# The seven forms of a swiglu's input at seven different rests of 512 bytes

## The chip, the cores and the metric

The kernel runs on one core of a Trainium2 chip. The metric is the device time of one execution in microseconds, the median over runs. A profile of one execution shows, for each engine, when every instruction ran. The engines are TensorE (PE for matmuls, PEld for the loads of their weights), VectorE (DVE), ScalarE (ACT), GpSimd (POOL) and SyncE (SP, which here only issues DMAs).

## The reference

A small streaming trunk: 256 tokens of width 2048, two layers, everything float32. Layer 0 mixes the tokens by gated linear attention, layer 1 by a sparse attention over a latent; after each mixer comes a swiglu. The change concerns the swiglus alone.

```python
def swiglu(h, w1, w3, w2):
    return (jax.nn.silu(h @ w1) * (h @ w3)) @ w2

def reference(x, ...):
    for i in range(DEPTH):              # DEPTH = 2
        h = rmsnorm(x, norm_mix[i])
        y = gla_mixer(h, ...) if i % 2 == 0 else dsa_mixer(h, ...)
        x = x + y
        x = x + swiglu(rmsnorm(x, norm_ffn[i]), ffn_w1[i], ffn_w3[i], ffn_w2[i])
    return rmsnorm(x, norm_final)
```

The matrices w1 and w3 are 2048 x 5632, w2 is 5632 x 2048.

## The kernel before

**Precision.** Each float32 product is made of three matmuls in the type float32r. A tile is split into a high part (a cast) and a low part (the rest), and the product is hi x wh + hi x wl + lo x wh. In every matmul the activations are the stationary operand, 128 x 128, and the weights the moving one, 128 x 512. So each group of three matmuls loads weights (in TensorE's sense) three times, from hi, hi and lo, and streams wh, wl and wh.

**Weights.** A block of 512 x 512 weights comes by a DMA of 1 MB into a buffer (raw, or one of v0, v1, v2, g3), ScalarE casts it to wh (line 137 in the feed-forward layers) and VectorE subtracts to get wl (line 138). There are three buffers each of wh and wl.

**Blocks of a swiglu.** The 5632 columns of w1 and w3 are 11 blocks of 512. Seven of them are made by a scheme of seven products (`pair`): h is cut into four parts by tokens and by width, and combinations of these parts, the *forms*, are multiplied with combinations of the weights. The forms are A11, F7, F5, A12, F6, F3 and N22. Each has a high and a low tile of 128 x 8 x 128 elements, 4096 bytes in each partition, made once per layer by `NormF.split` and kept for the layer. In `product` one pair of w blocks is multiplied with one form by 24 matmuls (line 397). The other four blocks use A11, F7, A12 and N22 only: one at the start (`plain`, line 468), three in pieces between the products (`plain_steps`, line 498). The second matrix w2 follows in pieces in between (`pieces`, lines 554 to 556). Their stationary tiles are g0 to g2.

**Where tiles stand.** A tile pool lays its tiles one behind another in the order in which their tags first appear. A pool named fz0 or fz1, opened for each swiglu, holds v0, the forms, the scratch tiles s1, y and w of the sums, v1 and v2. Every one of its tiles is a multiple of 2048 bytes in a partition, and the pool starts at byte 140800, which is 275 x 512. So in the kernel before all of them start at a multiple of 512 bytes: their *rest* of 512 is 0. The same holds for raw, wh, wl, g0 to g3 and for hh and hl, the high and low tiles of the mixers' inputs (lines 205 to 207). Tiles with other rests are found in the attention layer: its latent cth, ctl and its keys kih, kil at rest 192, its queries qh, ql at rest 320. With cth or ctl as stationary operand, the latent values (pv, lines 1027 to 1029, 512 columns) read whv and wlv, which lie in the buffers of wh and wl; the scores (psi, lines 920 to 922, and psl, lines 1046 to 1048, 256 columns) read qh and ql against kih, kil, cth and ctl.

**Order.** The order on each engine is that in which the code issues; what is put aside (transposes, scores and the like) is drawn into the stream of matmuls by `tick`.

Of the kernel before, what the change touches and what calls it, by code (L numbers as in the profile page):

```python
# [12 lines left out]
F32 = mybir.dt.float32  # L13
# [6 lines left out]
P = 128  # L20
# [35 lines left out]
def trunk(  # L56
# [219 lines left out]
    class NormF(Norm):  # L276
# [9 lines left out]
        def split(self, name, c, src, neg=False):  # L286
            if name not in self.forms:
                self.forms[name] = [self.pool.tile([P, 8, P], F32R, tag=f"{q}{name}", bufs=1, name=f"{q}{name}")
                                    for q in ("fh", "fl")]
            hi, lo = (z[:, 4 * c:4 * c + 4, :] for z in self.forms[name])  # L290
            if neg:
                nc.scalar.mul(hi, src, -1.0)
                nc.vector.scalar_tensor_tensor(lo, src, -1.0, hi.bitcast(F32), op0=ALU.mult, op1=ALU.subtract)
            else:
                nc.scalar.copy(hi, src)
                nc.vector.tensor_sub(lo, src, hi.bitcast(F32))
# [878 lines left out]
```

## Time and profile before

| | us |
|---|---|
| median of 2 runs | 2232.94 |
| lowest, highest | 2232.69, 2233.19 |
| profiled execution, from its first to its last instruction (span) | 2232.1 |
| layer 0, mixer and its output (0 to 395) | 395 |
| layer 0, swiglu (395 to 1080) | 685 |
| layer 1, mixer and its output (1080 to 1565) | 485 |
| layer 1, swiglu (1565 to 2160) | 595 |
| last block of w2 and the final norm | 72 |

The bounds of the stages are those of the first and last instructions of their lines, rounded. Of the profiled execution the profile gives the span alone; no time of its own stands beside it. [...] In rows of groups, the number behind x is the count, then come the busy time in us, the mean duration in ns and the idle time before.

### The profile page before, as it was taken

How to read it: one execution, taken by the hardware profiler on the slowest of the kernel's cores; microseconds unless marked ns; L12 is line 12 of the kernel's file. 1: busy time of each engine (PE TensorE's matmuls, PEld its weight loads, DVE VectorE, ACT ScalarE, POOL GpSimd, SP SyncE). 2: the span in 40 equal slices, each digit the busy share in tenths (PEclk: the TensorE clock that was granted, in tenths of full speed). 3: DMA queues.
4: the chain of work that ended last, by engine and by line, in shares of the span. 5: the costliest groups of instructions: out<-in, count | busy, mean ns of one | idle time of the engine just before them, and what ended most of it. 6: DMA issues, size and time to landing. Idle time of an engine off the chain costs nothing.

```text
span 2232.1 us, 25168 instructions
## 1 busy us (share of the span) xinstructions
PE 2217.3 (99%) x10247; PEld 1837.9 (82%) x10247; DVE 1577.6 (71%) x1282; ACT 1172.2 (53%) x1046; POOL 100.1 (4%) x147
## 2 busy tenths in 40 slices
PE   9999999999999999999999999999999999999998
PEld 8888888888888888888888888888888888888887
DVE  6546546778878878876555755556887887887874
ACT  5545445555555555555444444446555555555553
POOL 0000000000000000000100000000000000000000
PEclk9999999999999999999999999999999999999999
DMA  8555475597897898795554554467679779779763
GB/s 292 172 170 181 132 232 177 202 272 244 253 265 242 251 269 244 241 245 192 179 182 144 180 173 159 163 200 244 205 217 293 244 225 305 229 225 305 232 202 110
DMA packets 250547, 484.96 MB, mean 217 GB/s; under 512 B 8072, under 2 KB 20704, under 8 KB 250304
## 3 DMA queue, kind: packets, MB, share of 16 engines
q1 hardware_dynamic: 219856, 423.33, 55.1%
q0 software_dynamic: 29568, 58.72, 15.2%
q8 instruction: 80, 1.31, 0.2%
q10 hardware_dynamic: 1008, 1.31, 0.2%
q14 instruction: 35, 0.29, 0.0%
HBM read 481.20 MB, written 2.12 MB: 217 GB/s over the span
## 4 chain that ended last, share of the span: by engine, by line
PE 94%; DVE 2%; issue 1%; ACT 1%; DMA 1%; POOL 0%; POOLq 0%; ACTq 0%; DVEq 0%
PE acc L397 23%; PE acc L205 12%; PE acc L207 12%; PE acc L206 12%; PE half L498 11%; PE down L555 5%; PE down L556 5%; PE down L554 5%; PE acc L468 3%; PE tr L219 1%; DVE wl L138 1%; DMA g<-in_ffn_w 1%; PE trq L906 0%; PE po L765 0%; PE tr L253 0%
## 5 line engine op out<-in xcount | busy, mean ns | idle before, releaser
L196 DVE TENSOR_TENSOR wl<-raw,wh 128x2048 fp32r<-128x2048 f32 (+3 forms) x161 | 349.8, 2175 | 306.6 <-ACT wh L195 306.5
L137 ACT CAST wh<-raw 128x2048 fp32r<-128x2048 f32 x187 | 358.0, 1915 | 371.2 <-PE down L556 134.9
L138 DVE TENSOR_TENSOR wl<-raw,wh 128x2048 fp32r<-128x2048 f32 x187 | 427.1, 2289 | 160.2 <-ACT wh L137 159.9
L195 ACT CAST wh<-raw 128x2048 fp32r<-128x2048 f32 (+3 forms) x161 | 292.0, 1816 | 267.0 <-PE acc L207 211.1
L205 PE MATMUL acc<-wh,hh 128*128 128x512 f32 (+3 forms) x832 | 325.5, 391 | 0.0
L207 PE MATMUL acc<-wh,hl 128*128 128x512 f32 (+3 forms) x832 | 317.4, 381 | 0.0
L206 PE MATMUL acc<-wl,hh 128*128 128x512 f32 (+3 forms) x832 | 316.3, 380 | 0.6 <-DVE wl L196 0.6
L138 DVE TENSOR_TENSOR wl<-v,wh 128x2048 fp32r<-128x2048 f32 x102 | 232.8, 2288 | 34.2 <-ACT wh L137 34.1
L137 ACT CAST wh<-v 128x2048 fp32r<-128x2048 f32 x102 | 195.4, 1916 | 94.8 <-PE acc L397 54.9
L554 PE MATMUL down<-wh,g 128*128 128x512 f32 x512 | 200.0, 391 | 0.0
L556 PE MATMUL down<-wh,g 128*128 128x512 f32 x512 | 199.4, 389 | 0.0
L555 PE MATMUL down<-wl,g 128*128 128x512 f32 x512 | 199.3, 389 | 0.0
L206 PEld LDWEIGHTS acc<-wl,hh 128*128 128x128 f32 x832 | 156.7, 188 | 29.6 <-issue 1.7
L207 PEld LDWEIGHTS acc<-wh,hl 128*128 128x128 f32 x832 | 156.3, 188 | 29.5
L205 PEld LDWEIGHTS acc<-wh,hh 128*128 128x128 f32 x832 | 156.5, 188 | 28.4 <-issue 1.9
L397 PE MATMUL acc<-wh,fhF 128*128 128x512 f32 x448 | 175.1, 391 | 0.0
L397 PE MATMUL acc<-wh,flF 128*128 128x512 f32 x448 | 174.8, 390 | 0.0
L397 PE MATMUL acc<-wl,fhF 128*128 128x512 f32 x448 | 174.7, 390 | 0.0
L205 PE MATMUL acc<-wh,g 128*128 128x512 f32 x424 | 167.4, 395 | 0.0
L206 PE MATMUL acc<-wl,g 128*128 128x512 f32 x424 | 165.6, 391 | 0.0
L207 PE MATMUL acc<-wh,g 128*128 128x512 f32 x424 | 165.5, 390 | 0.0
L555 PEld LDWEIGHTS down<-wl,g 128*128 128x128 f32 x512 | 96.1, 188 | 20.1 <-DVE wl L138 0.4
(311 smaller groups left out, 3602.3 us busy)
## 6 DMA issues: line engine op xcount, KB each, us to landing
raw<-in_ffn_w SPq DMA_DIRECT2D x208, 1024.0 KB, 6.3
raw<-in_dsa_w_in SPq DMA_DIRECT2D x48, 1024.0 KB, 4.9
v<-in_ffn_w SPq DMA_DIRECT2D x42, 1024.0 KB, 8.3
raw<-in_gla_w_in SPq DMA_DIRECT2D x40, 1024.0 KB, 5.0
v<-in_ffn_w POOLq DMA_DIRECT2D x40, 1024.0 KB, 8.9
raw<-in_gla_w_out SPq DMA_DIRECT2D x16, 1024.0 KB, 5.0
g<-in_ffn_w POOLq DMA_DIRECT2D x16, 1024.0 KB, 12.5
raw<-in_dsa_w_out SPq DMA_DIRECT2D x16, 1024.0 KB, 4.9
```

The costliest lines, as they stand in the source:

```text
L137: nc.scalar.copy(wh, raw)
L138: nc.vector.tensor_sub(wl, raw, wh.bitcast(F32))
L195: a = nc.scalar.copy(wh[:, sl, :n], raw[:, sl, :n])
L196: v = nc.vector.tensor_sub(wl[:, sl, :n], raw[:, sl, :n], wh[:, sl, :n].bitcast(F32))
L205: nc.tensor.matmul(acc[t][:, :n], hi[:, k, ts_], wh[:, k, :n], start=start, stop=False)
L206: nc.tensor.matmul(acc[t][:, :n], hi[:, k, ts_], wl[:, k, :n], start=False, stop=False)
L207: nc.tensor.matmul(acc[t][:, :n], lo[:, k, ts_], wh[:, k, :n], start=False, stop=last)
L397: nc.tensor.matmul(acc, l_[:, k, :], r_[:, j, :], start=start and k == i == 0, stop=stop and k == 7 and i == 2, skip_group_check=not start)
L498: nc.tensor.matmul(acc[bank], l_[:, k, :], r_[:, j, :], start=start and k == i == 0, stop=stop and k == 7 and i == 2, skip_group_check=not ...
L554: nc.tensor.matmul(acc[t], hi[:, k, ts_], wh[:, k, :], start=start, stop=False)
L555: nc.tensor.matmul(acc[t], hi[:, k, ts_], wl[:, k, :], start=False, stop=False)
L556: nc.tensor.matmul(acc[t], lo[:, k, ts_], wh[:, k, :], start=False, stop=last)
```

## The change

When a form is first made, a tile of 16 float32 (64 bytes in a partition) that nothing uses is allocated behind its high and low tile, except behind the last form.

```diff
@@ class NormF, split(self, name, c, src, neg=False)
             if name not in self.forms:
                 self.forms[name] = [self.pool.tile([P, 8, P], F32R, tag=f"{q}{name}", bufs=1, name=f"{q}{name}")
                                     for q in ("fh", "fl")]
+                if len(self.forms) < 7:
+                    self.pool.tile([P, 16], F32, tag=f"rest{name}", bufs=1, name="rest")
             hi, lo = (z[:, 4 * c:4 * c + 4, :] for z in self.forms[name])
```

The instructions, their order on each engine and their waits are the same as before. What differs is where tiles start, in bytes of a partition (rest of 512 in brackets):

| tile | before | after |
|---|---|---|
| v0 | 140800 (0) | 140800 (0) |
| A11 high, low | 148992, 153088 (0) | the same (0) |
| s1 | 157184 (0) | 157248 (64) |
| F7 | 159232, 163328 (0) | 159296, 163392 (64) |
| v1 | 167424 (0) | 167552 (128) |
| y | 175616 (0) | 175744 (128) |
| F5 | 177664, 181760 (0) | 177792, 181888 (128) |
| w | 185856 (0) | 186048 (192) |
| A12 | 187904, 192000 (0) | 188096, 192192 (192) |
| F6 | 196096, 200192 (0) | 196352, 200448 (256) |
| F3 | 204288, 208384 (0) | 204608, 208704 (320) |
| N22 | 212480, 216576 (0) | 212864, 216960 (384) |
| v2 | 220672 (0) | 221056 (384) |
| wh, wl, raw, g0 to g3 | rest 0 | the same |

## The prediction

> **What bounds the kernel now.** I read the page first, then the busy time by stage, then the matmul rows of the feed-forward blocks, and last the chain of waits and the rows of single matmuls, since the change can only act through the cost of one instruction.
>
> ```profile
> span 2232.1 us, 25168 instructions
> PE 2217.3 (99%) x10247; PEld 1837.9 (82%) x10247; DVE 1577.6 (71%) x1282; ACT 1172.2 (53%) x1046; POOL 100.1 (4%) x147
> PEclk9999999999999999999999999999999999999999
> PE 94%; DVE 2%; issue 1%; ACT 1%; DMA 1%; POOL 0%; POOLq 0%; ACTq 0%; DVEq 0%
> ```
>
> TensorE is busy all the time, at the full granted clock, and the chain that ended last is TensorE for 94%. The two windows in which the feed-forward layers run:
>
> ```profile
> core 0: us, PE busy (x) PEld busy (x) DVE busy (x) ACT busy (x) POOL busy (x), PEclk, DMA share, GB/s
> 395.00:1080.00 685.00, 684.91 (x3076) 566.02 (x3075) 544.47 (x354) 378.77 (x268) 37.92 (x33) 1.00 0.81 241
> 1565.00:2160.00 595.00, 594.28 (x2659) 491.33 (x2658) 491.77 (x306) 330.69 (x210) 36.35 (x28) 1.00 0.83 246
> ```
>
> In 685 us TensorE has 0.1 us without a matmul in flight; VectorE is at 79%, ScalarE at 55%, the DMA engines at 81%. So a nanosecond on each matmul there is a nanosecond on the end, until VectorE or the DMAs are what is waited for, and those have about a fifth left.
>
> What one matmul costs shows in the chain, where a run of equal pieces is merged:
>
> ```profile
> 439.45 5.44 PE acc L397 x24
> 511.20 10.88 PE half L498 x48
> ```
>
> 10.88 us / 48 = 226.7 ns from one matmul to the next. A row's duration is longer because neighbours overlap; in an undisturbed run it is 389 ns, so a duration is about 162 ns over the spacing, and differences of durations are differences of spacing.
>
> **The change part by part.** It adds seven pads to the pool and no instruction: every engine has the same rows in the same order with the same waits, and no tile changes its size. Only the start addresses move. A11 stays at rest 0 of 512 bytes; F7 goes to 64, F5 to 128, A12 to 192, F6 to 256, F3 to 320, N22 to 384 (high and low half alike). With them move the scratch tiles s1, y and w and the weight buffers v1 (rest 128) and v2 (384). The moving operands of all these matmuls, wh and wl, stay at rest 0.
>
> How many matmuls read a moved form. The first three rows are those of line 397 (count, then shortest, median and longest duration in ns, first and last start), the others groups by shape (count, then busy us and mean ns). The views drop the digits: fhF is F7, F5, F6 and F3, fhA is A11 and A12, fhN is N22.
>
> ```profile
> L397 PE MATMUL acc<-wh,fhF x448: 387/389/481, 451.2 to 2134.2; 128*128 128x512 f32 x150
> L397 PE MATMUL acc<-wh,fhA x224: 389/389/389, 439.3 to 2112.4; 128*128 128x512 f32 x112
> L397 PE MATMUL acc<-wh,fhN x112: 387/389/396, 505.6 to 2145.1; 128*128 128x512 f32 x112
> ...
> L498 PE MATMUL half<-wh,fhA 128*128 128x512 f32 x192 | 75.1, 391 | 0.0
> L498 PE MATMUL half<-wh,fhF 128*128 128x512 f32 x96 | 37.9, 395 | 0.0
> L498 PE MATMUL half<-wh,fhN 128*128 128x512 f32 x96 | 37.3, 389 | 0.0
> ...
> L468 PE MATMUL acc<-wh,fhA 128*128 128x512 f32 x64 | 25.3, 396 | 0.2
> L468 PE MATMUL acc<-wh,fhF 128*128 128x512 f32 x32 | 12.6, 395 | 0.0
> L468 PE MATMUL acc<-wh,fhN 128*128 128x512 f32 x32 | 12.4, 389 | 0.0
> ```
>
> Each of these rows stands three times in its view (high form with wh, high form with wl, low form with wh). F: 3 x (448 + 96 + 32) = 1728. N22: 3 x (112 + 96 + 32) = 720. A: 3 x (224 + 192 + 64) = 1440, and the code uses A11 and A12 equally often, so 720 move. Together 3168 moved matmuls; 720 with A11 do not move.
>
> The price of a rest has to come from matmuls of this program whose two operands already stand at different rests. There is one place with the same shape: the latent values of the attention layer, whose stationary operand cth or ctl stands at rest 192 in the built program, while whv and wlv stand at rest 0. They run in the middle of an undisturbed stream:
>
> ```profile
> L1027 PE MATMUL pv<-whv,cth x16: 388/392/392, 1241.0 to 1412.1; 128*128 128x512 f32 x16
> L1028 PE MATMUL pv<-wlv,cth x16: 392/394/394, 1241.2 to 1412.3; 128*128 128x512 f32 x16
> L1029 PE MATMUL pv<-whv,ctl x16: 388/389/394, 1241.5 to 1412.6; 128*128 128x512 f32 x16
> ```
> ```profile
> 1407.32 0.39 PE L1027 MATMUL pv<-whv,cth 128*128 128x512 f32 x1
> ...
> 1408.69 0.39 PE L205 MATMUL acc<-wh,hh 128*128 128x512 f32 x1
> ...
> 1411.41 0.39 PE L1027 MATMUL pv<-whv,cth 128*128 128x512 f32 x1
> ...
> 1412.79 0.39 PE L205 MATMUL acc<-wh,hh 128*128 128x512 f32 x1
> ```
>
> Six matmuls from 1407.32 to 1408.69 and six from 1411.41 to 1412.79: 2.75 us / 12 = 229.2 ns, 2.5 ns over 226.7. The durations say the same: medians of 392, 394 and 389 where A11 and A12, at equal rests, have 389 as least, median and most over 224. So address rests do enter the time of a matmul, and at this distance they cost 1%.
>
> For other distances the trace has one lower row. With 256 columns, the attention scores stand 128 bytes apart (qh and ql at rest 320, kih, kil, cth and ctl at 192), the gated matmuls at equal rests:
>
> ```profile
> L206 PE MATMUL acc<-wl,hh 128*128 128x256 f32 x32 | 9.0, 283 | 0.0
> L1047 PE MATMUL psl<-ctl,qh 128*128 128x256 f32 x32 | 8.9, 280 | 0.0
> L922 PE MATMUL psi<-kih,ql 128*128 128x256 f32 x16 | 4.4, 278 | 0.0
> ```
>
> That is 3 to 5 ns less, in runs of three or six with other work between; I take 3 as the lower end, from the longer run. For the upper end I take matmuls at equal rests just after transposes or other small work, where the even beat is broken for some ten matmuls:
>
> ```profile
> L207 PE MATMUL acc<-wh,hl x3: 393/395/397, 1217.5 to 1218.9; 128*128 128x512 f32 x3
> ```
>
> 397 is 8 ns over 389. The value I use for all moved forms is +2.5 ns: same shape, same steady stream, and a distance that one of the forms (A12) gets exactly. The sum: 3168 x 2.5 ns = 7.9 us, all on TensorE's path. Against the profiled execution's span that is 2232.1 + 7.9 = 2240.0; the median of the two runs shown is 2232.94, 0.84 above the span, so 2240.8 us. The ends: 3168 x -3 ns = -9.5 us, 2223.4; 3168 x +8 ns = +25.3 us, 2258.2.
>
> The rest of the edit I cost at nothing. VectorE and ScalarE read v1, v2, s1, y and w elsewhere, with equal element counts, and in these stages they wait for TensorE; their cover is the fifth of idle time above. DMAs that land in v1 and v2 go to another rest:
>
> ```profile
> L137 ACT CAST wh<-v 128x2048 fp32r<-128x2048 f32 x102 | 195.4, 1916 | 94.8 <-PE acc L397 54.9 <-DMA v<-in_ffn_w 15.8 <-PE down L556 9.9
> ```
>
> ScalarE already waits 15.8 us for such landings, and none of it reaches TensorE. If this cover went, the late operand would be wh at line 397, after ScalarE's cast.
>
> [...]
>
> **The rivals.**
>
> *Nothing that can be seen.* The even beat of 226.7 may be a property of the pass and the 2.5 ns a disturbance of the short groups of six. For it: in the latent values the excess is not steady, one of three medians is 389. Against it: the matmuls on both sides of the group keep 389. Time: 2232.9, within 2 us.
>
> *A small gain.* If the 128-byte row is the typical one, 3168 x -3 to -5 ns: 2217 to 2223. Against it: 256 columns and broken runs.
>
> *A large gain.* Between 512 and 256 columns the duration falls by 389 - 283 = 106 ns, or 0.414 ns a column; 512 columns are 212 ns, and 14.7 ns of the 226.7 are a fixed part. If that part were a clash of two reads at equal rests and vanished at every other rest, 3168 x 14.7 ns = 46.6 us, 2186.3, just over 2%. Against it: rest 192 lost time. [...]
>
> *Slower by over 2%.* At some rest the weight load and the stream could block each other until the load is done. The price of a load that is not hidden is seen after the scores:
>
> ```profile
> 1216.97 0.48 PE L205 MATMUL acc<-wh,hh 128*128 128x512 f32 x1
> 1217.29 0.40 PE L206 MATMUL acc<-wl,hh 128*128 128x512 f32 x1
> ```
>
> 0.32 us instead of 0.227, 93 ns more. 2% is 44.7 us, so 480 such matmuls decide, fewer than F7, A12 or N22 have (720 each; 67 us, 2300). Against it: the one rest that can be seen costs 2.5, not 93.
>
> **How the numbers follow.** 2% is about what a measurement of this kernel tells from no change; its bounds are 2188.3 and 2277.6 us. Chances: a mild cost of about +2.5 ns, up to +8, 0.50; nothing to be seen 0.20; a small gain 0.19; a large gain 0.02; dearer than +8 ns 0.09, of it 0.06 beyond 2%. The predicted time is that of the likeliest, 2240.8. Its own range is 2235 to 2258; with no change and most of the small gain the range is 2223 to 2258, which leaves out some 0.18. Faster 0.02, same 0.92, slower 0.06.
>
> **What would show it.** Right: A11 keeps 389, the other forms get medians of 388 to 394 in a short repeating pattern, and the chain's 24-matmul pieces break up at 5.50 instead of 5.44 us; L554 to L556 and L205 to L207 do not move; TensorE stays busy throughout. N22 alone (rest 384) and the mixed F rows tell the rests apart. Wrong: moved forms at 389 mean rests do not matter; below 389, a gain by distance; a form at 400 or more, a rest that blocks; TensorE idle at L397 behind ScalarE's casts, the moved v1 and v2.

## The result and the profile after

The changed kernel takes 2247.07 us (median of two runs, 2246.93 and 2247.21), against 2232.94 before: a ratio of 1.0061 with a 95% interval of 1.0042 to 1.008. The forecast was 2240.8, within 2%, with a range of 2223 to 2258. The kernel is slower by 14.1 us, less than 2% but far outside the scatter of its runs; the spans of the two profiled executions differ by 13.0 us.

The page of the changed kernel, its span, the busy times and the engines' shares of the chain that ended last:

```profile
span 2245.1 us, 25168 instructions
PE 2231.1 (99%) x10247; PEld 1838.7 (82%) x10247; DVE 1580.4 (70%) x1282; ACT 1171.6 (52%) x1046; POOL 100.0 (4%) x147
PE 97%; DVE 1%; issue 1%; ACT 0%; DMA 0%; SPq 0%; POOL 0%; POOLq 0%; ACTq 0%
```

The same instructions, and TensorE's busy time is longer by 13.8 us (2231.1 against 2217.3) while no other engine's moves by more than 3. So all of the loss is time in which a matmul is in flight. In the windows of the two swiglus (busy time and count by engine, then clock and DMA) the same lengths of time hold fewer matmuls:

```profile
395.00:1080.00 685.00, 685.00 (x3041) 560.64 (x3040) 542.51 (x350) 373.43 (x261) 37.89 (x33) 1.00 0.80 239
1565.00:2160.00 595.00, 595.00 (x2629) 487.10 (x2628) 486.12 (x300) 327.06 (x207) 36.34 (x28) 1.00 0.82 241
```

There were 3076 and 2659 before: 35 and 30 fewer at the full granted clock, and 65 x 0.2267 us = 14.7 us (a little of it is the shift of the windows' content). TensorE has no gap left in them.

Which form pays how much shows in the chain of waits of the changed kernel (start, length, what), where each product of 24 matmuls with one form is one piece. The code multiplies with A11, F5, F3, A12, F6, F7 and N22 in this order, then A11 of the next pair (pieces between are left out):

```profile
439.74 5.46 PE acc L399 x24
...
451.63 5.57 PE acc L399 x24
457.21 5.52 PE half L500 x24
462.73 5.60 PE acc L399 x24
...
473.89 5.49 PE acc L399 x24
...
484.93 5.46 PE acc L399 x24
...
495.91 5.60 PE acc L399 x24
...
507.05 5.58 PE acc L399 x24
...
523.71 5.44 PE acc L399 x24
```

Before, every one of these pieces was 5.44 us. Now the length depends on the form, and the rest orders it. Divided by 24, less 5.44 / 24:

| form | rest | piece, us | over 5.44, ns a matmul | matmuls | us in all |
|---|---|---|---|---|---|
| A11 | 0 | 5.44 to 5.46 | 0 | 720 | 0 |
| F7 | 64 | 5.60 | 6.7 | 720 | 4.8 |
| F5 | 128 | 5.57 | 5.4 | 336 | 1.8 |
| A12 | 192 | 5.49 | 2.1 | 720 | 1.5 |
| F6 | 256 | 5.46 | 0.8 | 336 | 0.3 |
| F3 | 320 | 5.60 | 6.7 | 336 | 2.2 |
| N22 | 384 | 5.58 | 5.8 | 720 | 4.2 |

The last column sums to 14.8 us, against 13.0 by the spans and 14.1 by the medians. F6's 5.46 is no more than A11's first piece has, which follows a moved form. F7 and F3 (64 and 320) cost the same, F5 and N22 (128 and 384) nearly so: it looks as if only the start modulo 256 bytes counts. The pieces of line 500 mix two forms and lie at their mean: A11 with F7 is (5.44 + 5.60) / 2 = 5.52.

The rows of line 399 (shortest, median and longest duration) say it again. A11 and A12 share a row, so half of its matmuls are unmoved:

```profile
L399 PE MATMUL acc<-wh,fhF x448: 389/393/477, 451.5 to 2146.7; 128*128 128x512 f32 x150
L399 PE MATMUL acc<-wh,fhA x224: 388/389/398, 439.6 to 2124.6; 128*128 128x512 f32 x112
L399 PE MATMUL acc<-wh,fhN x112: 390/393/404, 506.9 to 2157.8; 128*128 128x512 f32 x112
```

And what was not moved did not change: the second matrix in after, then in before, and ScalarE's casts of the moved buffers in after (count, busy us, mean ns, then the idle time ahead of them and what ended it).

```profile
L556 PE MATMUL down<-wh,g 128*128 128x512 f32 x512 | 200.1, 391 | 0.0
```
```profile
L554 PE MATMUL down<-wh,g 128*128 128x512 f32 x512 | 200.0, 391 | 0.0
```
```profile
L137 ACT CAST wh<-v 128x2048 fp32r<-128x2048 f32 x102 | 194.8, 1910 | 98.6 <-PE acc L399 59.8 <-DMA v<-in_ffn_w 13.8 <-PE down L558 10.8
```

The casts take 1910 ns instead of 1916 and wait 13.8 us for DMAs instead of 15.8: nothing was lost at v1 and v2.

### The profile page after: what moved, and what is told of

Its sections match the earlier page's. It is cut to its first block, busy times and chain, and to the rows that moved or that the text cites. A ratio compares the mean times of both kernels' runs of the same rounds, so it can differ in the third digit from the quotient of the medians.

```text
span 2245.1 us, 25168 instructions
## 1 busy us (share of the span) xinstructions
PE 2231.1 (99%) x10247; PEld 1838.7 (82%) x10247; DVE 1580.4 (70%) x1282; ACT 1171.6 (52%) x1046; POOL 100.0 (4%) x147
## 4 chain that ended last, share of the span: by engine, by line
PE 97%; DVE 1%; issue 1%; ACT 0%; DMA 0%; SPq 0%; POOL 0%; POOLq 0%; ACTq 0%
PE acc L399 24%; PE acc L205 12%; PE acc L207 12%; PE acc L206 12%; PE half L500 12%; PE down L557 5%; PE down L558 5%; PE down L556 5%; PE acc L470 4%; PE tr L219 1%; PE trq L908 0%; PE po L767 0%; PE s L752 0%; PE po L1081 0%; PE tr L309 0%
## 5 line engine op out<-in xcount | busy, mean ns | idle before, releaser
L137 ACT CAST wh<-v 128x2048 fp32r<-128x2048 f32 x102 | 194.8, 1910 | 98.6 <-PE acc L399 59.8
L556 PEld LDWEIGHTS down<-wh,g 128*128 128x128 f32 x512 | 96.1, 188 | 20.3
```

The costliest lines, as they stand in the source:

```text
L137: nc.scalar.copy(wh, raw)
L556: nc.tensor.matmul(acc[t], hi[:, k, ts_], wh[:, k, :], start=start, stop=False)
```

## The experiments

The theory, from the table above (0 to 0.8 ns over 226.7 at rests 0 and 256, 2.1 to 6.7 at the others): a matmul of type float32r with 512 columns takes 226.7 ns in a stream when the starts of its stationary and its moving operand are equal modulo 256 bytes, and more otherwise; the whole loss is the sum of that over the moved forms. The rivals: the moved buffers v1, v2, s1, y and w do it; the rests themselves and not the distance between the operands; the period is 512; or the price is one of the place in the schedule (which product, which pieces) and not of the rest. The kernels before that ran beside these had medians of 2232.22 to 2233.74 us.

**All six at rest 256.** One pad of 256 bytes behind A11 moves the other six forms and all moved buffers to rest 256.

```diff
+                if name == "A11":
+                    self.pool.tile([P, 64], F32, tag=f"rest{name}", bufs=1, name="rest")
```

> One pad of 256 bytes behind A11: the other six forms, with s1, y, w, v1 and v2, all stand at rest 256. Theory (the price of a matmul goes by the distance of its two operands' starts, and repeats after 256 bytes): moved forms cost what F6 cost after the change, 0 to 0.5 ns each, so 0 to +1.5 us: 2233 to 2235, no change. Rival (the shifted weight buffers and scratch tiles carry part of the 14 us): slower by some 5 to 14 us, with TensorE idle or the casts later. Rival (period 512, F6's low price was due to its neighbours): 3168 x 2 to 6 ns, 2239 to 2252.

Measured: 2233.63 against 2233.74, ratio 1.0002 (0.9992 to 1.0011). In the rows of its line 399 the forms are back at a median of 389 (A11 and A12, not shown, have 389 throughout):

```profile
L399 PE MATMUL acc<-wh,fhF x448: 387/389/481, 451.0 to 2138.0; 128*128 128x512 f32 x150
L399 PE MATMUL acc<-wh,fhN x112: 388/389/398, 506.1 to 2148.9; 128*128 128x512 f32 x112
```

So a rest of 256 costs nothing that shows. With 64 and 320 both at 5.60 us a piece, and 128 and 384 at 5.57 and 5.58, the period is 256 bytes, not 512.

**All six at rest 64.** The same with a pad of 64 bytes.

```diff
+                if name == "A11":
+                    self.pool.tile([P, 16], F32, tag=f"rest{name}", bufs=1, name="rest")
```

> One pad of 64 bytes behind A11: the six other forms all at rest 64. Theory (each rest has its own price, 6.5 ns at 64): 3168 x 6.5 ns = 20.6 us, 2253.5, more than the whole change cost with mixed rests; every moved form has medians near 396, also F6, A12 and N22. Rival (the price belongs to the product in which a form stands, not to its rest): about the 14 us of the change again, 2247, with F6 still at 389.

Measured: 2254.05, ratio 1.0091 (1.0076 to 1.0106), 20.3 us more. In its chain F6's product, then N22's, and then 48 matmuls of A12 and N22:

```profile
485.74 5.60 PE acc L399 x24
...
508.03 5.60 PE acc L399 x24
513.63 11.20 PE half L500 x48
```

F6, which had 5.46 at rest 256, has F7's 5.60 here, and so has N22, which had 5.58 at rest 384, and A12 with it (11.20 / 48 = 233.3 ns). The price belongs to the rest, not to the form or to its place in the schedule. 3168 x 6.67 ns = 21.1 us; measured 20.3.

**Everything at rest 64.** A pad that stands ahead of all tiles grows by 64 bytes, so that forms, wh, wl, raw and buffers all move together.

```diff
-    cst.tile([P, 16], F32, name="pad")
+    cst.tile([P, 32], F32, name="pad")
```

> The pad ahead of all tiles is 64 bytes larger, no pads behind forms: every tile, stationary and moving alike, stands 64 bytes further, and no distance changes. Theory (the distance of the two operands counts): no change, 2233 within 2 us. Rival (the rest of the stationary operand counts by itself): 9024 matmuls of 512 columns x 6.5 ns = 59 us, 2292. Rival (the rest of the moving operand counts as well): any change between.

Measured: 2232.37 against 2233.74, ratio 0.9996 (0.9987 to 1.0006). Its chain has the pieces of before:

```profile
451.60 5.44 PE acc L397 x24
457.04 5.44 PE half L498 x24
```

So it is the distance between the two operands that counts; a rest of 64 is as good as 0 when both have it.

**The moving operand at rest 64.** The forms stay at rest 0, and wh and wl go to 64, which reaches the matmuls of the mixers and of w2 as well.

```diff
+    wp.tile([P, 4, NB], F32, tag="raw", bufs=RAW, name="raw")
+    wp.tile([P, 16], F32, tag="rest", bufs=1, name="rest")
...
-    sm.tile([P, 40], F32, tag="pad", bufs=1, name="pad")
+    sm.tile([P, 24], F32, tag="pad", bufs=1, name="pad")
```

> Only the moving operands move: wh and wl stand at rest 64, all forms, hh, hl and g at rest 0 as before. Theory (signed distance, stationary less moving, modulo 256, so -64 is 192): all but the latent values' 8976 matmuls of 512 columns pay what A12 paid, 2.8 ns: 25 us, 2258. Rival (distance without sign, 64 either way): 6.5 ns each, 58 us, 2291. Rival (only the stationary operand's own rest counts): no change, 2233.

Measured: 2249.23, ratio 1.007 (1.0053 to 1.0087): 15.5 us more. The sign was expected, the size was not. In its chain, N22's product and the 48 that follow:

```profile
508.82 5.49 PE acc L400 x24
514.31 11.00 PE half L501 x48
```

That is A12's 5.49 at rest 192, 228.8 to 229.2 ns. The distance has a sign: stationary less moving is -64, and modulo 256 that is 192. At 2.1 ns the 3888 matmuls with forms (A11 now among them) give 8.2 us; the other 7 us lie in the mixers and w2, with 3 x (736 + 424 + 512) = 5016 matmuls of 512 columns: 1.4 ns each, less than the forms; that it is because other work breaks their streams is a guess.

**Each distance by itself.** In front of the trunk stand groups of 48 equal matmuls with one stationary and one moving tile, which nothing uses; its 2620.69 us hold them too. A group's name gives distance d, columns n, stationary width m, and r for float32r or h for bfloat16.

```diff
+        def run(m, dist, n=NB, reps=48, mv=mov, sv=stat, e=4):
...
+            for _ in range(reps):
+                nc.tensor.matmul(ps[0:m, 0:n], sv[:, o:o + m], mv[:, 0:n], start=True, stop=True)
```

> The kernel before, with a probe ahead of it that adds work and changes no output: groups of 48 equal matmuls, one stationary tile and one moving tile, the start of the stationary slice 0 to 320 bytes behind rest 0, then the same with fewer stationary columns (64, 32), fewer moving columns (384, 256) and bfloat16 operands. Theory (two reads of TensorE meet in SBUF, with a period of 256 bytes): spacing 226.7 ns at distance 0 and 256, about 233 at 64 and 320, 232 at 128, 229 at 192; the excess falls with fewer stationary columns, as the weight load is shorter, and does not fall with fewer moving columns. Rival (the excess is one of addresses alone, whatever is read): the same excess with 32 stationary columns. Rival (rests below 64 bytes are free, a line of 64 bytes is the unit): 226.7 at 4 to 48. The whole run is some 450 us longer than before, by the probe.

Rows of single groups (shortest, median, longest duration, then first and last start):

```profile
L1114 PE MATMUL d64n512m128r<-mov,stat x48: 392/393/398, 72.6 to 83.6; 128*128 128x512 f32 x48
L1114 PE MATMUL d128n512m128r<-mov,stat x48: 392/396/398, 117.4 to 128.3; 128*128 128x512 f32 x48
L1114 PE MATMUL d192n512m128r<-mov,stat x48: 388/392/394, 162.0 to 172.8; 128*128 128x512 f32 x48
L1114 PE MATMUL d256n512m128r<-mov,stat x48: 388/389/389, 206.3 to 216.9; 128*128 128x512 f32 x48
L1114 PE MATMUL d64n512m64r<-mov,stat x48: 388/396/399, 239.4 to 250.4; 128*64 128x512 f32 x48
L1114 PE MATMUL d128n512m64r<-mov,stat x48: 389/390/397, 250.6 to 261.4; 128*64 128x512 f32 x48
L1114 PE MATMUL d64n512m32r<-mov,stat x48: 388/392/397, 272.7 to 283.6; 128*32 128x512 f32 x48
L1114 PE MATMUL d64n384m128r<-mov,stat x48: 336/338/338, 303.2 to 311.6; 128*128 128x384 f32 x48
L1114 PE MATMUL d0n256m128r<-mov,stat x48: 278/283/290, 328.5 to 334.1; 128*128 128x256 f32 x48
L1114 PE MATMUL d192n256m128r<-mov,stat x48: 279/279/284, 345.6 to 351.1; 128*128 128x256 f32 x48
L1114 PE MATMUL d0n512m128h<-movb,statb x48: 379/379/390, 351.3 to 361.4; 128*128 128x512 bf16 x48
L1114 PE MATMUL d64n512m128h<-movb,statb x48: 379/379/379, 361.6 to 371.8; 128*128 128x512 bf16 x48
```

First to last start are 47 steps. The exact starts give 233.2 ns at 64, 233.4 at 128, 228.9 at 192 and 226.7 at 256; at 0 and at 240, once the stream had settled, 226.7. Of the other distances between 4 and 224 all but 8 and 176 cost 5 to 8 ns; these two cost 4.0 and 3.2. So the rival that small distances are free has fallen: 4 bytes already cost 5.8 ns.

Three more things are to be seen. With a stationary operand half as wide, whose load takes 134 ns instead of 188, the spacing is 230.2, 232.8 and 229.3 ns at 0, 64 and 128; with a quarter it is 231.4, 231.6 and 230.7. So the narrower the operand, the less the distance matters, as the theory had it, but narrow operands pay 3.5 to 4.8 ns at equal starts, where the full one pays nothing, and that the theory did not have. With fewer moving columns the price does change, against the theory: with 384 unequal starts cost 3.3 ns at 64, 2.6 at 128 and nothing at 192 (173.3 at 0). With 256 the sign turns round: unequal starts are *quicker* than equal ones, by 2 to 4 ns in the duration (279 to 281 at 64, 128 and 192 against 283) and 1 to 2 ns from start to start. And bfloat16 does not depend on the distance at the four that were tried (0, 64, 128 and 192): a median of 379 at each, 215.9 ns from start to start.

**Odd multiples of 32.** The first pad has 32 bytes and the later ones 64, so that the forms come to 32, 96, 160, 224, 288 and 352.

```diff
+                if len(self.forms) < 7:
+                    n = 8 if len(self.forms) == 1 else 16
+                    self.pool.tile([P, n], F32, tag=f"rest{name}", bufs=1, name="rest")
```

> Pads so that F7 stands at rest 32, F5 at 96, A12 at 160, F6 at 224, F3 at 288 and N22 at 352. Theory (price by distance, period 256): F3 pays what F7 pays and N22 what F5 pays; with values between the neighbours (32: 3, 96: 6, 160: 4, 224: 1.5 ns) 2.2 + 2.0 + 2.9 + 0.5 + 1.0 + 4.3 = 13 us, 2246. Rival (only multiples of 64 bytes differ): 32 costs what 0 costs, and so on: 0 + 2.2 + 3.9 + 0.9 + 0.1 + 4.7 = 12 us, but F3 at 389 and N22 at 396. Rival (some odd rest is below the price of rest 0): a form under 389 ns.

Measured: 2253.9 against 2233.67, ratio 1.009 (1.0075 to 1.0105). The size was missed. Six of the seven products in its chain, A11 first (F7's, between F6's and N22's, has 5.60 too):

```profile
440.05 5.44 PE acc L400 x24
...
451.90 5.61 PE acc L400 x24
...
463.08 5.60 PE acc L400 x24
...
474.29 5.60 PE acc L400 x24
...
485.49 5.59 PE acc L400 x24
...
507.73 5.62 PE acc L400 x24
```

F5 at 96 (451.90), F3 at 288 (463.08), A12 at 160 (474.29), F6 at 224 (485.49) and N22 at 352 (507.73) all pay 6 to 8 ns. Both rivals have fallen: the odd multiples of 32 are not free, and none is below rest 0. So 192 is a dip of its own, and a price cannot be read off between two neighbouring rests: 224 lies between 192 (2.1) and 256 (0) and pays 6.2 ns (5.59 us the piece).

**The buffers alone.** Pads put v1 and y at rest 128 and v2 at 384, with every form at rest 0 or 256.

```diff
+                if name == "N22":
+                    self.pool.tile([P, 32], F32, tag="rest2", bufs=1, name="rest")
...
+                if j:
+                    self.pool.tile([P, 32], F32, tag="rest0", bufs=1, name="rest")
...
+            if c == 0:
+                self.pool.tile([P, 32], F32, tag="rest1", bufs=1, name="rest")
```

> Only what is not a form stands off: v1 and y at rest 128, v2 at 384, as after the change; F7 stays at 0 and the five later forms stand at 256. Theory (the forms carry all of it): 2233 to 2235, no change. Rival (casts, differences and transfers on moved buffers carry a part): up to the 1.1 us by which the change's 14.1 exceeds the 13.0 of its span, or more: 2235 to 2240.

Measured: 2232.76 against 2233.67, ratio 0.9997 (0.9987 to 1.0006); the 24-matmul pieces of its chain are 5.44 again, such as N22's:

```profile
505.46 5.44 PE acc L403 x24
```

The rests of v1, y and v2 cost nothing that shows (the interval ends 1.3 us above the kernel before), and the rival that the 14 us come from the casts and sums on ScalarE and VectorE has fallen. The scratch tiles s1 and w stand at 0 and 256 here; their rests after the change, 64 and 192, were not tried by themselves.

**Finer steps, also for a gain.** The same kind of probe in steps of 4 bytes from 196 to 256, and with narrower operands, whose loads are shorter (148 ns at 80 columns against 188 at 128). If some distance lay below 226.7 ns, a kernel faster than both would exist.

```diff
+        run(P, 204)
+        run(P, 208)
+        run(P, 212)
...
+        run(80, 0)
+        run(P, 0, 508)
```

> The kernel before with a second probe ahead of it (work added, no output changed): groups of 48 matmuls at distances 196 to 252 bytes in steps of 4, then distance 0 with 124, 112, 96 and 80 stationary columns and with 508, 504, 496, 480 and 448 moving columns, last 24 plain float32 matmuls at distances 0 and 64. [...] Theory B (distance 0 is the end of a slope, and a distance between 240 and 256 is better still): some group between 216 and 226 ns, which would be worth up to 9024 x 10 ns = 90 us in the whole kernel. [...] Plain float32, whose weights were loaded long before its stream ends, shows the same time at both distances.

```profile
L1114 PE MATMUL d204n512m128r<-mov,stat x48: 389/389/393, 39.6 to 50.3; 128*128 128x512 f32 x48
L1114 PE MATMUL d212n512m128r<-mov,stat x48: 392/398/402, 61.6 to 72.8; 128*128 128x512 f32 x48
L1114 PE MATMUL d240n512m128r<-mov,stat x48: 387/391/392, 139.6 to 150.4; 128*128 128x512 f32 x48
L1114 PE MATMUL d252n512m128r<-mov,stat x48: 389/389/390, 173.0 to 183.6; 128*128 128x512 f32 x48
L1114 PE MATMUL d0n512m80r<-mov,stat x48: 390/395/400, 216.9 to 227.8; 128*80 128x512 f32 x48
L1114 PE MATMUL d0n504m128r<-mov,stat x48: 386/388/388, 239.0 to 249.7; 128*128 128x504 f32 x48
```

No group of 512 columns comes below 226.7 ns, so theory B and its gain have fallen; and the way up to 256 is not even. Single distances reach the 226.7 (204, 228, 252), and between them others pay as much as 10 ns (212: 236.7). The two probes do not agree everywhere: the distance 240 had 389 as median in the first and has 391 here (1.6 ns over 226.7 from start to start), and 208 cost 6.6 ns there and costs 5.3 here. What makes the difference was not tried; the groups stand in another order. 504 columns take the same 226.7 as 512, though from 480 to 504 the spacing rises by 3.3 ns for every 8 columns. A stationary operand of 80 columns pays 6.5 ns at equal starts, so the shorter load does not help there either. In plain float32 both distances tried, 0 and 64, have the same mean duration, 592 ns. Nothing tried here beats the kernel before, and the hope of a gain was given up.

**All six at 192, all six at 128.** The two prices that the forecast had weighed against one another, each by itself: a pad of 48 and of 32 float32 behind A11.

```diff
+                    self.pool.tile([P, 48], F32, tag=f"rest{name}", bufs=1, name="rest")
```

> One pad of 192 bytes behind A11: the six other forms all at rest 192, the rest from which the prediction took its +2.5 ns. Theory (the price by distance): 3168 x 2.2 to 2.8 ns = 7.0 to 8.9 us, 2240 to 2242, with durations cycling through 388, 392 and 394; the prediction's sum was right for this rest and wrong only in taking it for the others. Rival (the latent values' price does not carry over to long streams): 2233, or 2250 and more.

```diff
+                    self.pool.tile([P, 32], F32, tag=f"rest{name}", bufs=1, name="rest")
```

> One pad of 128 bytes behind A11: the six other forms all at rest 128. Theory (the price by distance, from F5 after the change and the probe): 3168 x 5 to 6.8 ns = 16 to 21 us, 2249 to 2254. Rival (the 256-column rows at this distance carry over to 512 columns): 3168 x -3 ns, 2223 to 2233.

Measured at 192: 2238.61 against 2233.12, ratio 1.0024 (1.0014 to 1.0034). At 128: 2250.72, ratio 1.008 (1.0062 to 1.0098). N22's product and the 48 after it, first at 192, then at 128:

```profile
506.60 5.49 PE acc L399 x24
512.09 10.99 PE half L500 x48
```
```profile
507.40 5.58 PE acc L399 x24
512.98 11.14 PE half L500 x48
```

At 192 the whole kernel loses 5.5 us, 1.7 ns for each of the 3168 matmuls (2.1 in the undisturbed pieces), less than the 7.0 to 8.9 us that were expected; at 128 it loses 17.6 us, 5.6 ns each, as expected. Had all forms gone to the rest from which the price was taken, the forecast of +7.9 us would have been 2.4 us too high.

## Why the prediction came out as it did

**What bounds the kernel: right.** A nanosecond on each matmul of the swiglus went to the end. TensorE's busy time grew by 13.8 us and the span by 13.0, and VectorE, ScalarE and the DMAs took no part.

**The mechanism: right.** The forecast said that "address rests do enter the time of a matmul", from the latent values alone, and the first rival, nothing that can be seen, is out: only matmuls with a moved form changed, and only when the distance to their moving operand changed (everything moved together: ratio 0.9996).

**The count: right.** 3168 matmuls are touched. (The forecast speaks of seven pads; the condition `len(self.forms) < 7` makes six in each swiglu. The rests that it lists are right.) With all of them at 64 the loss was 20.3 us, or 6.4 ns each, which fits the 6.7 of the pieces.

**The price: mis-sized.** The step that failed is "The value I use for all moved forms is +2.5 ns". The reason given for it was true of A12 alone ("a distance that one of the forms (A12) gets exactly"): at 192 the pieces show 2.1. But 192 and 256 are the two cheap rests of the six. The other four, with 2112 of the 3168 matmuls, cost 5.4 to 6.7. The mean is 13.0 us / 3168 = 4.1 ns by the spans (4.5 ns by the medians' 14.1 us), so the term was 13.0 to 14.1 and not 7.9 us. The forecast had one price and six distances, and no row of before with 512 columns told how the price goes with the distance; the odd multiples of 32 then showed that it could not have been interpolated either. That one price came as near as it did is partly luck: two cheap rests among the six pulled the mean down.

**The ends of the range.** The lower end, -3 ns, came from the attention scores with 256 columns at a distance of 128. The sign was read rightly (281 against 283 in the probe at this distance, 1.3 ns from start to start), but it does not carry over to more columns: in the same probe this distance costs 2.6 ns with 384 and 6.7 with 512. The upper end, +8 ns from the broken beat, was not reached by any form. The result lies between the two.

**The offset.** The forecast took 0.84 us from the span to the time. In every run listed here time less span is 1.7 to 2.0 us; the median and the span of before were of different executions. Of the 6.3 us by which the forecast was low, 5.1 are the price and the rest is this.

**The rivals.** The small gain and the large gain fell by sign. The large gain rested on a fixed part of 14.7 ns that might vanish at unequal starts; the probes found nothing under 226.7 for 512 columns of this type at any distance tried. The load that is not hidden (+93 ns) did not occur: the dearest distance found costs 10.

**What stays open.** Why it depends on the distance. That two reads meet, and a shorter load meets less, was the author's guess; no run shows the reads themselves. The narrow operands speak for it in part: from equal starts to a distance of 64 the spacing rises by 6.6 ns with 128 stationary columns, by 2.6 with 64 and by 0.2 with 32. Against it, they paid at equal starts too (3.5 and 4.8 ns). It was not tried whether the moving operand's own layout, or the PSUM bank, shifts the pattern; the runs show times only, not what the chip does inside.

## What to carry to other kernels

Where float32r matmuls of 512 columns fill TensorE, keep the starts of stationary and moving operand equal modulo 256 bytes of a partition, and make any pad a multiple of 256: in these runs a matmul took 226.7 ns from start to start at distances 0 and 256, and 228.8 to 233.4 at 64, 128 and 192, up to 3% more, which no idle time showed (the dearest distance of the probes, 212, took 236.7). Look for it in the length of a long undisturbed piece of the chain divided by its count, and compare pieces whose operands stand differently. These runs show it for stationary operands of 128 columns; with 256 moving columns the sign turned (durations of 279 to 281 ns at unequal starts, 283 at equal ones). A price seen at one distance or one number of columns should not be used for another; measure the distance in question by 48 matmuls in a row.

## What the runs showed that was not expected

- The sign turns with the number of columns: at 256 columns the unequal starts tried save 1 to 2 ns a matmul in the probe, at 512 unequal starts cost up to 10.
- The pattern is not smooth: 204, 228 and 252 bytes take the 226.7 ns of 0, 212 costs 10 ns and 224 costs 6.7.
- The slower kernels scatter less. The kernel before ran from 2231.97 to 2236.96 us in 13 runs, the kernel at rest 192 from 2238.38 to 2239.60 in ten, that at rest 128 from 2250.55 to 2250.91 in four, that at rest 64 from 2253.81 to 2254.32. One profiled execution of the kernel at rest 256 (span 2235.9) shows what the scatter may be: TensorE waits 2.0 us for a late wl ahead of this row, where in the changed kernel TensorE has no gap in the swiglus.

```profile
L399 PE MATMUL acc<-wl,fhN 128*128 128x512 f32 x112 | 43.8, 391 | 2.0 <-DVE wl L138 2.0
```
